# Moving the start addresses of SBUF tiles in a two-block transformer kernel: the small-column pool ahead of the split-weight pool, and filler tiles in three places

## The chip, the cores and the metric

The kernel runs on one core of a Trainium2 chip. The metric is the device time in microseconds (us) of one execution. Three executions of the kernel before gave 2179.43 us (median), from 2176.91 to 2179.5. The execution that was profiled took 2180.57 us, and its trace spans 2178.5 us of that.

## The reference

The input is 256 tokens of width 1024 in float32. Two layers and a further block follow each other:

```python
for layer in range(DEPTH):                 # DEPTH = 2
    mixer = hgrn_gmlp_mixer if layer % 2 == 0 else mla_moba_mixer
    x = x + mixer(x, *mixer_params[layer])
    x = x + peer_ffn(x, *ffn_params[layer])
...
def peer_ffn(x, norm_ffn, w_query, sub_keys, expert_down, expert_up):
    ...
        q = (xi @ w_query).reshape(B, PEER_CHUNK, PEER_HEADS, 2, PEER_HALF)
        s = jnp.einsum('bthpd,hpnd->bthpn', q, sub_keys)
        ...                                # two top-16, then the top 16 of the pairs
        u = jnp.take(expert_down, idx, axis=0)
        act = jax.nn.gelu(jnp.einsum('btd,bthkd->bthk', xi, u).astype(jnp.float32))
        v_sel = jnp.take(expert_up, idx, axis=0)
        return jnp.einsum('bthk,bthkd->btd', (g * act).astype(xi.dtype), v_sel)
```

Each peer layer has 16,384 experts. The second block (`second_block`) normalises, multiplies by a wide input matrix, does a pooled branch and a dilated attention, and multiplies by two projections and an output matrix.

## The kernel before

**Products in three parts.** Every large matrix product is done on fp32r operands split into a high and a low part: `hi = copy(x)` on ScalarE (L487) and `lo = x - hi` on VectorE or GpSimd (L488), in `split_weights`. A product then takes three matmuls (hi·hi, hi·lo, lo·hi, in `mm3`), so TensorE reads two SBUF operands for each: the stationary one, 128 columns (512 bytes of a partition), which a weight load brings in, and the moving one, 256 or 512 columns. All of them are issued from one line, L421.

**Peer layers.** The kernel doesn't gather experts. It takes all 128 blocks of 128 experts in turn. For each block `project` multiplies the block's down weights by the normalised tokens: 24 matmuls, named `ps<-xh,wh`, `ps<-xl,wh`, `ps<-xh,wl` in the trace, with the weights stationary and the tokens (`xh`, `xl`) moving, 256 columns. `expand` multiplies the gated activations by the block's up weights: 12 matmuls, `acc<-wh,W` and `acc<-wl,W`, with the activations `W` stationary and the weights moving, 512 columns. Per layer the stretches are: the query product (`acc<-xh,w`, `acc<-xl,w`) with the top-16 searches on VectorE and the first 40 projections between them; the gate matrices from one-hot products in fp16 (`acc<-oo,ah`) with 60 more projections; 124 expansions, into whose last part the other 28 projections are put one by one; and 4 expansions from tiles named `places`. The order within a stretch is written out by the program, partly by a count of costs (class `Balance`), and is fixed before the run.

**Mixers and second block.** Their products stream through the class `Stream`: a piece of 1024 weight columns is loaded into `wraw`, split, and used. In "T" jobs the weights are stationary and the tokens move (`acc<-xh,wh`); in "N" jobs the tokens are stationary and the weights move (`acc<-wh,xh`, 256 or 512 columns). The mixers put some split pieces in their own pool (`w`, names `wh` and `wl` as well) and some in the shared pool `ws`.

**Pools.** SBUF is given out in the order in which pools are opened. The outer order is constants (with `xh` and `xl`), `raw` (4 tiles of 4096 bytes), `ws` (5 pairs `wh`, `wl` of 4096 bytes each), `esm` (four tags of one or a few columns), and then what each stage opens. In a peer layer's front that is `small`, `wraw`, `tmp` and `w` (the split query weights); in the second block `first`, `wraw`, `small`, `mg` (two tiles), `act` and `wk`. A tile takes its bytes rounded up to 32.

Of the kernel before, what the change touches and what calls it, by code (L numbers as in the profile page):

```python
# [7 lines left out]
F32 = mybir.dt.float32  # L8
# [101 lines left out]
class Lin:  # L110
# [5 lines left out]
    def __init__(self, x, W, nk, cols, cn, kind, cb, late=0, k0=0, acc=None, start=True, stop=True,  # L116
                 need=None, mid=None, of=None, pieces=None):
        self.x, self.W, self.nk, self.cn, self.kind, self.cb, self.late = x, W, nk, cn, kind, cb, late
        self.mid, self.of = mid, of
        self.pieces = pieces or range({"T": cn // 128, "N": 2, "N2": 4}[kind])  # L120
        self.k0, self.acc, self.start, self.stop, self.need = k0, acc, start, stop, need
        self.cols = cols if isinstance(cols, tuple) else (cols, cn, 1, cn)
        self.w, self.keep = [], False
        if of:
            of.keep = True
# [240 lines left out]
class Net:  # L366
    def __init__(self, ctx, tc, A):
        self.tc, self.nc, self.A, self.ctx = tc, tc.nc, A, ctx
        nc = self.nc
        P = lambda name, **k: ctx.enter_context(tc.tile_pool(name=name, **k))  # L370
        self.cp = P("consts", bufs=1)
        self.raw = P("raw", bufs=4)
        self.dram = P("dram", bufs=1, space=DRAM)
        self.n = 0
        cp = self.cp
        self.ws = P("ws", bufs=WS)
        self.pa = P("pa", bufs=4, space=PSUM)
        self.pb = P("pb", bufs=4, space=PSUM)
        self.esm = P("esm", bufs=1)
        self.xn = [cp.tile([128, KB, S], F32R, name=n) for n in ("xh", "xl")]  # L380
        self.ident = cp.tile([128, 128], F32, name="ident")
        nc.scalar.dma_start(self.ident, A["c_ident"])
        self.vec = cp.tile([128, NVEC], F32, name="vec")
        self.entry = self.brow = None
# [701 lines left out]
    def peer(self, l, nxt, parity):  # L1086
# [8 lines left out]
        T = lambda pool, shape, dt, name, tag=None, **k: pool.tile(shape, dt, name=self.uid(name), tag=tag or name, **k)  # L1095
        with ExitStack() as outer:
# [49 lines left out]
            with ExitStack() as ctx:  # L1146
                P = lambda name, **k: ctx.enter_context(tc.tile_pool(name=self.uid(name), **k))
# [76 lines left out]
                def pair_top(tb):  # L1224
# [15 lines left out]
                        hs = range(h, h + 4)  # L1240
                        yield from best16([CV[:, j] for j in hs], [CI[:, j] for j in hs], [cand[:, j] for j in hs], 112)
                    gt = T(tmp, [128, 8, 16], F32, "gt")
                    gs = T(self.sm, [128, 8], F32, "gs")
                    nc.vector.tensor_tensor(gt, CV, CV[:, :, 0:1].to_broadcast([128, 8, 16]), op=OP.subtract)
                    nc.scalar.activation(gt, gt, AF.Exp)

# [47 lines left out]
                def front():  # L1294
# [51 lines left out]
                    for tb in range(2):  # L1346
                        yield from pair_top(tb)
# [23 lines left out]
            with ExitStack() as ctx:  # L1371
                P = lambda name, **k: ctx.enter_context(tc.tile_pool(name=self.uid(name), **k))
# [201 lines left out]
    def block2(self, out):  # L1574
# [5 lines left out]
                    pass  # L1580
        with ExitStack() as ctx:
            P = self.open(ctx)
            xp = P("mg", bufs=1)
            a = P("act", bufs=1)
            wk = P("wk", bufs=2)
            W = A["w_in_2"][0]
# [300 lines left out]
```

## Time and profile before

| | |
|---|---|
| median of three executions | 2179.43 us |
| the profiled execution | 2180.57 us |
| its span in the trace | 2178.5 us |
| TensorE busy | 2122.6 us, 97% |
| VectorE busy | 1568.8 us, 72% |
| ScalarE busy | 1125.7 us, 52% |
| GpSimd busy | 215.7 us, 10% |
| mean DMA rate | 175 GB/s |
| granted TensorE clock, mean | 0.994 |

Busy times are of the engine, and can hide spacing: matmuls are pipelined, and a matmul's own time in the trace is longer than the distance to the next one. So for TensorE the distance between the starts of two matmuls that follow each other says what one costs, and it is read from the view of instructions in order of time. "PEld" is the weight load, which overlaps the matmuls.

### The profile page before, as it was taken

The page shows a single profiled execution, that of the slowest core. Times are in us where ns is not written, and L with a number is a line of the kernel's source. Part 1 is how long each engine was busy: PE and PEld are TensorE (multiplying, and loading weights), DVE is VectorE, ACT ScalarE, POOL GpSimd, SP SyncE. Part 2 cuts the span into 40 slices and gives each one's busy share as a digit, 9 for nine tenths or more (in the row PEclk, how much of TensorE's full clock was granted, in tenths as well). Part 3 has the DMA queues.
Part 4 walks back from the last instruction along what each step waited for, and adds up shares of the span by engine and source line. Part 5 has one row for each costly group of instructions (what it writes and reads, how often), then busy time and mean ns, then how long its engine had stood idle before and what let it go on. Part 6 is the DMA issues. An engine that isn't in the chain of part 4 may idle for free.

```text
span 2178.5 us, 37618 instructions
## 1 busy us (share of the span) xinstructions
PE 2122.6 (97%) x14793; PEld 1932.1 (89%) x14793; DVE 1568.8 (72%) x2898; ACT 1125.7 (52%) x1944; POOL 215.7 (10%) x133
## 2 busy tenths in 40 slices
PE   7899999999999999998999999999999999999998
PEld 6879999999888888987799999998888889899998
DVE  7968978997555565668679789986666656644565
ACT  6245655554444444557455655555555555554443
POOL 2520110000000000013202200000000000122223
PEclk9999999999999999999999999999999999999999
DMA  7555454455666665744264545446666657475443
GB/s 233 185 185 184 145 194 146 156 159 161 188 189 190 188 195 192 260 129 148 87 233 135 195 149 162 155 155 188 189 187 190 194 193 261 148 218 153 136 146 115
DMA packets 165581, 382.19 MB, mean 175 GB/s; under 512 B 13137, under 2 KB 82444, under 8 KB 165148
## 3 DMA queue, kind: packets, MB, share of 16 engines
q1 hardware_dynamic: 160544, 364.95, 53.0%
q0 software_dynamic: 4672, 14.76, 1.9%
q8 instruction: 116, 1.90, 0.4%
q14 instruction: 61, 0.50, 0.1%
q10 hardware_dynamic: 188, 0.09, 0.0%
HBM read 376.56 MB, written 8.43 MB: 177 GB/s over the span
## 4 chain that ended last, share of the span: by engine, by line
PE 86%; DVE 9%; ACT 3%; issue 1%; DMA 0%; DVEq 0%; ACTq 0%
PE acc L421 53%; PE ps L421 29%; DVE wl L488 2%; ACT wh L487 1%; PE bsc L421 1%; PE bo L421 1%; DVE qL L678 1%; PE ps L200 1%; PE sc L421 0%; PE bpt L1747 0%; DVE eq L1278 0%; DVE s L1195 0%; DVE CI L1200 0%; DVE SC L658 0%; ACT scr L873 0%
## 5 line engine op out<-in xcount | busy, mean ns | idle before, releaser
L488 DVE TENSOR_TENSOR wl<-raw,wh 128x1024 fp32r<-128x1024 f32 x484 | 600.0, 1249 | 135.2 <-ACT wh L487 134.4
L421 PE MATMUL acc<-wh,W 128*128 128x512 f32 x1984 | 630.8, 395 | 0.0
L421 PE MATMUL ps<-xh,wh 128*128 128x256 f32 x2048 | 579.1, 283 | 0.0
L421 PE MATMUL ps<-xl,wh 128*128 128x256 f32 x2048 | 572.9, 280 | 0.0
L421 PE MATMUL ps<-xh,wl 128*128 128x256 f32 x2048 | 572.6, 280 | 0.0
L487 ACT ACTIVATE wh<-raw 128x1024 fp32r<-128x1024 f32 x504 | 526.9, 1054 | 74.2 <-PE ps L421 55.4
L421 PEld LDWEIGHTS acc<-wh,W 128*128 128x128 f32 x1984 | 373.4, 188 | 85.6 <-DVE W L1431 0.4
L421 PE MATMUL acc<-wl,W 128*128 128x512 f32 x992 | 391.5, 395 | 0.0
L421 PEld LDWEIGHTS ps<-xh,wh 128*128 128x128 f32 x2048 | 385.2, 188 | 2.4
L421 PEld LDWEIGHTS ps<-xl,wh 128*128 128x128 f32 x2048 | 385.1, 188 | 2.1
L421 PEld LDWEIGHTS ps<-xh,wl 128*128 128x128 f32 x2048 | 385.2, 188 | 0.0
L421 PEld LDWEIGHTS acc<-wl,W 128*128 128x128 f32 x992 | 186.7, 188 | 42.0 <-DVE wl L488 0.3
L1430 ACT ACTIVATE W<-ZB 128x256 fp32r<-128x256 f32 x168 | 91.4, 544 | 184.7 <-PE acc L421 161.0
L487 ACT ACTIVATE wh<-wraw 128x1024 fp32r<-128x1024 f32 (+1 forms) x140 | 144.4, 1043 | 46.5 <-PE acc L421 38.2
L1431 DVE TENSOR_TENSOR W<-ZB,W 128x256 fp32r<-128x256 f32 x168 | 89.8, 534 | 108.4 <-ACT W L1430 108.4
L488 DVE TENSOR_TENSOR wl<-wraw,wh 128x1024 fp32r<-128x1024 f32 (+2 forms) x104 | 132.8, 1284 | 45.9 <-ACT wh L487 45.7
L421 PE MATMUL acc<-xh,wh 128*128 128x256 f32 x480 | 136.2, 284 | 0.0
L421 PE MATMUL acc<-xh,wl 128*128 128x256 f32 x480 | 133.4, 278 | 0.0
L421 PE MATMUL acc<-xl,wh 128*128 128x256 f32 x480 | 133.3, 278 | 0.0
L181 POOL TENSOR_TENSOR ZB<-X,gain 128x512 f32<-128x512 f32 x4 | 5.2, 1293 | 1293.9 <-ACT ZB L179 1293.9
L1474 ACT ACTIVATE ZB<-acc 128x352 f32<-128x352 f32 (+30 forms) x128 | 47.7, 373 | 123.1 <-PE acc L421 119.3
L421 PE MATMUL acc<-wh,xh 128*128 128x256 f32 (+2 forms) x336 | 107.9, 321 | 0.9 <-ACT scr L873 0.9
(409 smaller groups left out, 3114.2 us busy)
## 6 DMA issues: line engine op xcount, KB each, us to landing
raw<-in_l_down_t_dram SPq DMA_DIRECT2D x256, 512.0 KB, 4.3
raw<-in_l_peer_expert_up_dram SPq DMA_DIRECT2D x248, 512.0 KB, 4.3
wraw<-in_l_w_in_dram SPq DMA_DIRECT2D x36, 512.0 KB, 5.1
wraw<-in_w_in_dram SPq DMA_DIRECT2D x36, 512.0 KB, 3.9
wraw<-in_l_peer_w_query_dram SPq DMA_DIRECT2D x32, 512.0 KB, 5.3
wraw<-in_w_in_dram SPq DMA_DIRECT2D x48, 256.0 KB, 3.3
wraw<-in_l_w_out_dram SPq DMA_DIRECT2D x16, 512.0 KB, 4.2
brow<-row POOLq DMA_DIRECT2D x1, 5120.0 KB, 33.6
```

Source lines behind the costliest of these rows:

```text
L181: nc.gpsimd.tensor_tensor(y, x, self.gB[:, ns], op=OP.mult)
L200: nc.tensor.transpose(q[:, k * 128:k * 128 + 128], self.work[tb][:, (k0 + k) * 128:(k0 + k) * 128 + 128], self.net.ident)
L421: self.nc.tensor.matmul(*a, **k)
L487: self.nc.scalar.activation(hi, r, AF.Copy)
L488: (eng or self.nc.vector).tensor_tensor(lo, r, hi.bitcast(F32), op=OP.subtract)
L678: nc.vector.tensor_tensor(qL, q, Wt, op=OP.mult)
L1430: nc.scalar.activation(h, act, AF.Copy)
L1431: nc.vector.tensor_tensor(l, act, h.bitcast(F32), op=OP.subtract)
L1474: nc.scalar.activation(ZB[:, f - E0:, t4], pv[:, f:], AF.Copy, scale=1.0 / GSC)
```

## The change

Nothing is added to or taken from the instructions, and on no engine does one stand in another place. What changes is where tiles lie in SBUF.

```diff
         cp = self.cp
+        self.esm = P("esm", bufs=1)
         self.ws = P("ws", bufs=WS)
         self.pa = P("pa", bufs=4, space=PSUM)
         self.pb = P("pb", bufs=4, space=PSUM)
-        self.esm = P("esm", bufs=1)
...
-                    gs = T(self.sm, [128, 8], F32, "gs")
+                    gs = T(self.sm, [128, 32], F32, "gs")[:, :8]
...
             P = self.open(ctx)
+            P("gap1", bufs=1).tile([128, 48], F32, name="gap1")
             xp = P("mg", bufs=1)
+            P("gap2", bufs=1).tile([128, 96], F32, name="gap2")
             a = P("act", bufs=1)
```

The pool `esm` takes 128 bytes of a partition, so `ws` starts 128 bytes later, and what is behind both stays. `gs` has four buffers in `small`, each now 128 bytes and not 32: what is opened behind `small` in a peer layer's front moves by 384 bytes. In the second block `mg` moves by 192 bytes, and `act` and `wk` by 576. The first bytes in the built programs, and what is left of them after division by 256 (the "offset" below):

| tiles | before | after | offset before | offset after |
|---|---|---|---|---|
| `xh`, `xl` | 16512, 24704 | same | 128 | 128 |
| `raw` (4) | 33600 and on | same | 64 | 64 |
| `ws`: `wh`, `wl` | 49984 and on | 50112 and on | 64 | 192 |
| `W` (activations) | 135104, 137152 | same | 192 | 192 |
| `places` | 91072 | same | 192 | 192 |
| mixers' pool `w` | 134080 and on | same | 192 | 192 |
| query weights `w` | 196672 and on | 197056 and on | 64 | 192 |
| `mgh`, `mgl` | 124480, 132672 | 124672, 132864 | 64 | 0 |
| `bh`, `bl`, `yh`, `yl` | 157248 and on | 157824 and on | 64 | 128 |

Every piece of these tiles that a matmul reads starts a multiple of 256 bytes behind the tile's start, so the offset is that of each operand.

## Rows read from the trace of the kernel before

**Rows 1.** The page: busy time of the engines, and the last chain's shares.

```profile
PE 2122.6 (97%) x14793; PEld 1932.1 (89%) x14793; DVE 1568.8 (72%) x2898; ACT 1125.7 (52%) x1944; POOL 215.7 (10%) x133
...
PE 86%; DVE 9%; ACT 3%; issue 1%; DMA 0%; DVEq 0%; ACTq 0%
```

**Rows 2.** Groups by shape on TensorE: count | busy us, mean ns | idle before.

```profile
L421 PE MATMUL acc<-wh,W 128*128 128x512 f32 x1984 | 630.8, 395 | 0.0
L421 PE MATMUL ps<-xh,wh 128*128 128x256 f32 x2048 | 579.1, 283 | 0.0
...
L421 PE MATMUL acc<-xh,wh 128*128 128x256 f32 x480 | 136.2, 284 | 0.0
...
L421 PE MATMUL acc<-wh,xh 128*128 128x256 f32 x256 | 74.9, 293 | 0.9 <-ACT scr L873 0.9
...
L421 PE MATMUL acc<-xh,w 128*128 128x256 f32 x384 | 71.1, 281 | 0.0
```

**Rows 3.** Stretches: length, busy PE, PEld, DVE, ACT, POOL (count), clock, DMA share, GB/s.

```profile
200.00:300.00 100.00, 94.11 (x789) 93.56 (x787) 95.48 (x337) 53.93 (x76) 19.27 (x7) 0.98 0.43 138
...
350.00:500.00 150.00, 150.00 (x1457) 149.00 (x1455) 139.00 (x233) 78.67 (x183) 0.00 (x0) 1.00 0.50 156
...
560.00:800.00 240.00, 240.00 (x1035) 194.58 (x1034) 142.20 (x173) 117.67 (x172) 0.00 (x0) 1.00 0.62 189
...
810.00:940.00 130.00, 130.00 (x836) 117.42 (x835) 79.32 (x98) 65.96 (x96) 0.00 (x0) 1.00 0.66 217
...
1940.00:2100.00 160.00, 159.34 (x1274) 147.84 (x1273) 85.44 (x142) 78.24 (x137) 36.78 (x20) 1.00 0.51 150
```

**Rows 4.** Waits of TensorE: total us, times, longest.

```profile
PE ps L1267 <- DVE gt L1264: 7.4, 4, 2.4
```

**Rows 5.** In order of time, TensorE: start us, own us; projections, 42 spacings apart.

```profile
401.00 0.28 PE L421 MATMUL ps<-xl,wh 128*128 128x256 f32 x1
...
405.95 0.28 PE L421 MATMUL ps<-xl,wh 128*128 128x256 f32 x1
```

**Rows 6.** The same view, first mixer, weights from pool `w`: 47 spacings apart.

```profile
29.36 0.28 PE L421 MATMUL acc<-xh,wh 128*128 128x256 f32 x1
...
34.69 0.28 PE L421 MATMUL acc<-xh,wl 128*128 128x256 f32 x1
```

**Rows 7.** Second mixer, N job; weights of `ws`, then from 991.25 of `w`: 6, 11 spacings.

```profile
990.57 0.28 PE L421 MATMUL acc<-wh,xh 128*128 128x256 f32 x1
...
991.25 0.28 PE L421 MATMUL acc<-wh,xh 128*128 128x256 f32 x1
...
992.55 0.28 PE L421 MATMUL acc<-wh,xl 128*128 128x256 f32 x1
```

**Rows 8.** Expansions, 66 spacings from the first row's start to the last's.

```profile
589.64 0.62 PE L421 MATMUL acc<-wh,W 128*128 128x512 f32 x2
...
604.97 0.40 PE L421 MATMUL acc<-wh,W 128*128 128x512 f32 x1
```

**Rows 9.** The last expansions of a layer, from `places`: start, length of all, count.

```profile
1883.94 9.70 PE L421 MATMUL acc<-places 128*128 128x512 f32 x42
```

**Rows 10.** Second block's end: projections (15 spacings), then a T job (47).

```profile
2137.10 0.28 PE L421 MATMUL acc<-bh,wh 128*128 128x256 f32 x1
...
2138.90 0.28 PE L421 MATMUL acc<-xh,wh 128*128 128x256 f32 x1
...
2144.44 0.28 PE L421 MATMUL acc<-xh,wl 128*128 128x256 f32 x1
```

**Rows 11.** Projections in the first layer's search stretch, 76 spacings.

```profile
290.01 0.28 PE L421 MATMUL ps<-xl,wh 128*128 128x256 f32 x1
...
298.63 0.28 PE L421 MATMUL ps<-xh,wl 128*128 128x256 f32 x1
```

**Rows 12.** Groups on VectorE: the split in `ws`, and in `places`.

```profile
L488 DVE TENSOR_TENSOR wl<-raw,wh 128x1024 fp32r<-128x1024 f32 x484 | 600.0, 1249 | 135.2 <-ACT wh L487 134.4 <-PE ps L421 0.3
...
L488 DVE TENSOR_TENSOR places<-ZB,places 128x1024 fp32r<-128x1024 f32 x8 | 9.8, 1219 | 0.0
```

## The prediction

> **What bounds the kernel now.** I read the page first: TensorE is busy for 97% of the span, and 86% of the chain that ended last runs on it [rows 1]. Then the view by stretches [rows 3]: in the gate stretch (350 to 500), the expansions (560 to 800), the alternating stretch (810 to 940) and the second block (1940 to 2100) TensorE is busy throughout or nearly, and VectorE is busy for 139.00 of 150, 142.20 of 240, 79.32 of 130 and 85.44 of 160 us. So there a cheaper matmul shortens the run. In the search stretch (200 to 300) it is otherwise: VectorE 95.48 of 100 us, TensorE 94.11, and TensorE waits for search results there, the gates `gt` for example [rows 4].
>
> The view that decides this case is TensorE's in order of time. No instruction changes place, so the change can act only through addresses, and addresses differ already within the kernel before. With "difference" I mean the stationary operand's offset less the moving one's, modulo 256 bytes. Matmuls of 256 columns at steady spacing, with offsets from the table of the change:
>
> - moving 128, stationary 64, difference 192: 4.95 us for 42 spacings, 117.9 ns [rows 5]
> - moving 128, stationary 192, difference 64: 5.33 us for 47, 113.4 ns [rows 6]
> - moving 64, stationary 64, difference 0: 1.80 us for 15, 120.0 ns; the T job right behind it (difference 192) takes 5.54 us for 47, 117.9 ns [rows 10]
> - in one unbroken chain, weights of `ws` (moving 64, stationary 128, difference 64) run at 0.68 us for 6, 113.3 ns, and the next unit, from pool `w` (moving 192, difference 192), at 1.30 us for 11, 118.2 ns [rows 7]
>
> With 512 columns: the expansions (moving 64, stationary 192, difference 128) take 15.33 us for 66, 232.3 ns [rows 8]; those from `places` (both 192, difference 0) take 9.70 us for 42, and less the last one's own 0.39 us (as long as the 395 ns of the others of this shape), 9.31/41 = 227.1 ns [rows 2, 9].
>
> So the spacing follows the difference, though not it alone: the same addresses that give 117.9 ns once ran for 76 spacings at 8.62/76 = 113.4 ns [rows 11]. A chain of matmuls falls into one step or the other when it starts and tends to keep it; the difference sets which step it mostly ends in.
>
> The other engines show nothing like this: VectorE's split takes a mean of 1249 ns in `ws` and 1219 ns in `places`, whose tiles lie at another offset [rows 12], 2% apart. I cost VectorE, ScalarE, GpSimd and the DMAs at nothing; they are covered by TensorE outside the search stretch in any case.
>
> **The change part by part.** It removes and adds no instruction and no wait. The counts are from rows 2 and the loops.
>
> 1. Expansions: `ws` goes to 192, the difference from 128 to 0, the pair of offsets that `places` has. Two of three read `wh`, so 1984 × 3/2 = 2976 matmuls [rows 2], each 232.3 − 227.1 = 5.2 ns cheaper: 15.5 us. VectorE's 142.20 of 240 us leave this room.
> 2. Projections: 3 × 2048 = 6144 [rows 2], from difference 192 to 64, the pair of rows 6: at most 117.9 − 113.4 = 4.5 ns each. Some already run fast [rows 11], and some chains will stay slow, so I take 3.5 ns in long chains. The gate stretches hold 2 × 60 × 24 = 2880: 10.1 us. VectorE limits this: 150 us there become 150 − 1080 × 0.0035 = 146.2 for TensorE (some 1080 of the 1457 matmuls are projections; the rest are fp16 and don't change), against 139.00 on VectorE [rows 3]; it fits with 5% left, and I keep 90%: 9.1 us. The alternating stretches hold 2 × 28 × 24 = 1344 in chains of 24, which start anew at each expansion: 1344 × 3.1 = 4.2 us. The search stretches hold 2 × 40 × 24 = 1920, and with the query products, which move in the same way (1.5 × 384 = 576) [rows 2], 2496 × 3.5 = 8.7 us. There VectorE sets the pace, so a faster TensorE mostly waits earlier for `gt`; I keep 40%: 3.5 us.
> 3. T jobs, nearly all in the second block: 3 × 480 less 144 that read pool `w` is 1296, from difference 192 to 64. Their bounds are 0 (they already run fast) and 1296 × 4.5 = 5.8 us; stretches of both kinds stand in the trace, so half: 2.9 us.
> 4. The second block's projections and output product: 2 × 192, from difference 0 to 64 (`bh`, `yh` moving at 128; `mg` stationary at 0 under `ws` at 192): 120.0 − 113.4 = 6.6 ns, 2.5 us. That is what the two fillers there are for.
> 5. Against it: N jobs on `ws` go from difference 64 to 192, as in rows 7. Of the 3 × 256 [rows 2] 408 read `ws`: at most 408 × 4.9 = 2.0 us dearer, and since some are slow now, I take 1.3 us. 240 of 512 or 448 columns make the same move; no row shows that. Their bound is the spread of rows 8 and 9, 5.2 ns either way, ±1.2 us; I take 0.
> 6. Mixers' output products that move `ws` weights past tokens at 192: about 138 × 5.2 = 0.7 us cheaper, as in 1. The fp32 transposes are too few to count (±0.3 us).
>
> The sum: 15.5 + 9.1 + 4.2 + 3.5 + 2.9 + 2.5 − 1.3 + 0.7 = 37.1 us. From the profiled 2180.57 us (span 2178.5 and 2.1 around it), which lies 1.1 us above the median of 2179.43, that gives 2143.5, and from the median 2142.3. I say 2142.
>
> **The rivals.**
>
> *Addresses make no difference; the spacings come from the kind of job.* For it: each class of offsets belongs to other operations, and rows 11 run fast without any change. Against it: in rows 7 one job, one shape and one chain change step with the buffer alone. It would give 2179. The Trainium skill has the rule behind this rival: SBUF — State Buffer, section "Who interferes with whom", gives TensorE two independent read ports, one for the moving operand and one for weight loads, and says "PE and ACT never wait on anyone". By that rule the sum is zero; rows 7 disagree with it by 4.9 ns a matmul.
>
> *Only part of it arrives.* Chains stay in the slow step (in chains of 24 and 48 that start anew after the fp16 products or an expansion), or VectorE takes over: at 139.00 of 150 us [rows 3] the rise of its share late in the gate stretch could meet TensorE's new pace. Then parts 2 and 3 give about 4 us together, and the others stay: 15.5 + 4 + 2.5 + 0.7 − 1.3 = 21.4, thus 2158.
>
> *All of it arrives.* Every chain of the gate and alternating stretches and of the T jobs ends in the fast step, (2880 + 1344 + 1296) × 4.5 = 24.8 us, and half of the search stretch's 2496 × 4.5 counts, 5.6 us, with parts 1, 4, 5, 6 as above: 15.5 + 24.8 + 5.6 + 2.5 − 1.3 + 0.7 = 47.8, thus 2132.
>
> *Slower.* Difference 0 is the worst one at 256 columns [rows 10]; `places` may be fast for how its chain is entered [rows 9], as rows 11 are. If an expansion paid at 512 columns what 256 columns pay twice, 2 × 120.0 = 240.0 ns, 2976 × 7.7 = 22.9 us would be added. With chains that keep their step (parts 2 and 3 at 0) only part 4 stands against it: 2179.4 + 22.9 − 2.5 = 2200. It decides once the expansions' spacing is over 232.3 + 2.5/2.976 = 233.1 ns and the projections don't move. Against it: the 42 of rows 9 hold 227.1 ns as a whole, first ones included, at both operands' new offsets.
>
> **How the numbers follow.** The forecast 0.71; part of it 0.14; all of it 0.05; no difference 0.06; slower 0.04. A measurement of this kernel can tell about 0.2%, 4.4 us, from no change. Faster by more than that is 0.90, within it 0.06, slower 0.04. The range from 2131 to 2157 takes in the forecast with its bounds (parts 2 and 3 between half and all), the case of all, and not quite that of part; outside lie the other cases and about 0.06 of the forecast's own, together close to 0.2. All cases but two are of one sign, so one range is enough.
>
> **What would show it.** In the profile after, expansions should stand 227 ns apart, and the 240 us from 560 hold about 1035 × 232.3/227.1 = 1059 matmuls; projections in the gate stretch 113 to 114 ns apart, with a few chains at 118; the second block's `acc<-wh,mgh` at 113 in place of 120; N jobs on `ws` at 118. The waits for `gt` and for search results should grow, since TensorE arrives earlier: that is where part 2 loses its 60%. VectorE's busy time should stay within 1%. I am wrong in part 1 if expansions stay over 230 ns; in part 2 if most long chains of projections stay at 118, or if TensorE waits for VectorE in the gate stretch; and wrong altogether if all spacings stay as they are.

## The result, and the profile after

The changed kernel takes 2153.68 us (median of four, 2152.74 to 2157.69) against 2179.47 for the kernel before (four, 2176.91 to 2179.76): the ratio is 0.9888, 95% interval 0.9871 to 0.9905, so 25.8 us faster. The forecast was 2142 with a range from 2131 to 2157: sign and range hold, 11.3 of the 37.1 us did not come.

The page of the changed kernel, busy times and the last chain's shares, and its groups by shape on TensorE and VectorE (count | busy us, mean ns | idle before), against [rows 1, 2, 12]:

```profile
PE 2104.1 (98%) x14793; PEld 1930.2 (90%) x14793; DVE 1565.5 (73%) x2898; ACT 1124.5 (52%) x1944; POOL 217.9 (10%) x133
...
PE 86%; DVE 10%; ACT 3%; issue 1%; DMA 0%; ACTq 0%; DVEq 0%
...
L488 DVE TENSOR_TENSOR wl<-raw,wh 128x1024 fp32r<-128x1024 f32 x484 | 598.6, 1246 | 137.4 <-ACT wh L487 136.3
L421 PE MATMUL acc<-wh,W 128*128 128x512 f32 x1984 | 619.5, 389 | 0.0
L421 PE MATMUL ps<-xh,wh 128*128 128x256 f32 x2048 | 582.1, 284 | 0.0
```

The work on every engine is the same, and TensorE is busy for 18.5 us less, the other engines for at most 3.3 us less: the larger of the expansions' two groups gives 11.3 of the 18.5, the projections' group shown here nothing. VectorE's split kept its time (1249 and 1246 ns).

Stretches of the changed kernel (columns as in [rows 3]):

```profile
560.00:780.00 220.00, 220.00 (x972) 182.24 (x971) 133.62 (x162) 110.57 (x162) 0.00 (x0) 1.00 0.64 194
350.00:500.00 150.00, 150.00 (x1459) 148.93 (x1458) 138.80 (x231) 78.25 (x183) 0.00 (x0) 1.00 0.51 158
```

The kernel before has 949 matmuls between 560 and 780 us:

```profile
560.00:780.00 220.00, 220.00 (x949) 178.36 (x948) 130.16 (x159) 108.10 (x158) 0.00 (x0) 1.00 0.62 188
```

972 in place of 949 is a step shorter by 2.4%, as from 232.6 to 227 ns. In the gate stretch 1459 stand where 1457 stood: next to nothing moved there. The instructions in order of time (start, own time) say the same. The changed kernel's expansions, 69 spacings:

```profile
589.03 0.62 PE L421 MATMUL acc<-wh,W 128*128 128x512 f32 x2
...
604.67 0.62 PE L421 MATMUL acc<-wh,W 128*128 128x512 f32 x2
```

15.64/69 = 226.7 ns, 232.3 in [rows 8]. A pair of projections in its gate stretch, from the fp16 products to the next ones:

```profile
403.26 1.09 PE L421 MATMUL acc<-oo,ah 128*128 128x128 f16 x16
404.16 0.36 PE L421 MATMUL ps<-xh,wh 128*128 128x256 f32 x1
404.36 0.28 PE L421 MATMUL ps<-xl,wh 128*128 128x256 f32 x1
...
409.77 0.28 PE L421 MATMUL ps<-xh,wl 128*128 128x256 f32 x1
409.90 1.09 PE L421 MATMUL acc<-oo,ah 128*128 128x128 f16 x16
```

From 404.36 to 409.77 are 46 spacings, 117.6 ns: the step of [rows 5], with the addresses of [rows 6], which ran at 113.4. And in the search stretch of the same trace, at the same addresses, two chains follow each other:

```profile
284.70 0.28 PE L421 MATMUL ps<-xh,wl 128*128 128x256 f32 x1
...
295.25 0.28 PE L421 MATMUL ps<-xh,wl 128*128 128x256 f32 x1
296.89 0.41 PE L1289 MATMUL ps<-ident,sel 128*128 128x128 f32 x2 [1.37 <-DVE sel L1283]
...
297.38 0.28 PE L421 MATMUL ps<-xh,wl 128*128 128x256 f32 x1
...
322.46 0.28 PE L421 MATMUL ps<-xh,wl 128*128 128x256 f32 x1
```

93 spacings in 10.55 us are 113.4 ns; then, after a pause and two transposes, 213 in 25.08 us are 117.7. So at difference 64 both steps exist, as they do at 192 [rows 5, 11].

Summed over every matmul of a kind, the time from its start to the next start went so (us, before to after; only spacings without a gap are compared in parts 5 and 6):

| part of the prediction | forecast | in the traces |
|---|---|---|
| 1 expansions | -15.5 | 692.5 to 675.2: -17.3 |
| 2 projections and query | -16.8 | 742.8 to 741.7 and 68.5 to 67.3: -2.3 |
| 3 T jobs | -2.9 | 172.2 to 171.3: -0.9 |
| 4 second block | -2.5 | 46.4 to 45.0: -1.4 |
| 5 N jobs | +1.3 | 768 x (116.6 - 116.1 ns) = +0.4; of 512 or 448 columns 213 x (224.0 - 227.0) = -0.6 |
| 6 mixers' output products | -0.7 | 160 x (228.3 - 231.7) = -0.5 |

Together -22.6, and the span went from 2178.5 to 2155.6, -22.9. The profiled execution is the longest of its four (2157.69), so the traces hold 22.9 of the median's 25.8 us. The gaps that parts 5 and 6 leave out moved single groups by up to 3.5 us, both ways, and all but cancel.

### The profile page after: what moved, and what is told of

The parts are those of the page before. It is cut to its first block, busy times and chain, and to the rows that moved or that the text cites. A ratio compares the mean times of both kernels' runs of the same rounds, so it can differ in the third digit from the quotient of the medians.

```text
span 2155.6 us, 37618 instructions
## 1 busy us (share of the span) xinstructions
PE 2104.1 (98%) x14793; PEld 1930.2 (90%) x14793; DVE 1565.5 (73%) x2898; ACT 1124.5 (52%) x1944; POOL 217.9 (10%) x133
## 4 chain that ended last, share of the span: by engine, by line
PE 86%; DVE 10%; ACT 3%; issue 1%; DMA 0%; ACTq 0%; DVEq 0%
PE acc L421 53%; PE ps L421 29%; DVE wl L488 3%; ACT wh L487 1%; PE bsc L421 1%; PE bo L421 1%; DVE qL L678 1%; PE ps L200 1%; PE sc L421 0%; DVE s L1195 0%; PE lev L421 0%; PE bpt L1749 0%; DVE CI L1200 0%; ACT scr L873 0%; ACT TF L1227 0%
## 5 line engine op out<-in xcount | busy, mean ns | idle before, releaser
L488 DVE TENSOR_TENSOR wl<-raw,wh 128x1024 fp32r<-128x1024 f32 x484 | 598.6, 1246 | 137.4 <-ACT wh L487 136.3
L421 PE MATMUL acc<-wh,W 128*128 128x512 f32 x1984 | 619.5, 389 | 0.0
L421 PEld LDWEIGHTS ps<-xl,wh 128*128 128x128 f32 x2048 | 390.5, 191 | 2.0
L421 PE MATMUL acc<-wl,W 128*128 128x512 f32 x992 | 386.0, 389 | 0.0
L488 POOL TENSOR_TENSOR wl<-wraw,wh 128x1024 fp32r<-128x1024 f32 (+1 forms) x36 | 87.0, 2418 | 222.8 <-ACT wh L487 215.5
```

Source lines behind the costliest of these rows:

```text
L421: self.nc.tensor.matmul(*a, **k)
L488: (eng or self.nc.vector).tensor_tensor(lo, r, hi.bitcast(F32), op=OP.subtract)
```

## The experiments

Theory A is the prediction's: the difference sets the spacing. Theory C: the difference sets which steps there are, and what TensorE does ahead of a chain sets which of them it takes. Rivals: addresses don't matter; the absolute place matters; the place in the program does. A "chain" is a run of projections with nothing else between; "slow" and "fast" are its steps of 117.7 and 113.4 ns. One trace of each kernel was kept, so whether a kernel takes the same steps in every execution no run shows.

**Which edit brings the gain.** `ws_only` has the pool's move alone:

```diff
+        self.esm = P("esm", bufs=1)
         self.ws = P("ws", bufs=WS)
...
-        self.esm = P("esm", bufs=1)
```

> The change with only the pool of short columns moved in front of the split weights; gs keeps its 8 columns and the second block has no fillers. Theory A (the spacing of 512-column matmuls follows the difference of the operands' start offsets, and the expansions go from 128 to 0): the 2976 expansions run at 227 ns again instead of 232.6, about -17 us, and the projections hardly move, so about -19 to -22 us of the change's -25.8: near 2158 us against 2179. Theory B (the fillers carry a good part of the gain): at most -15 us, above 2164. In both the projections stay near 117.5 ns.

Measured: 2154.85 us, ratio 0.9893 (0.9875 to 0.9910); expansions 226.8 ns, projections 116.8.

`rest_only` has the rest:

```diff
+                    gs = T(self.sm, [128, 32], F32, "gs")[:, :8]
...
+            P("gap1", bufs=1).tile([128, 48], F32, name="gap1")
+            P("gap2", bufs=1).tile([128, 96], F32, name="gap2")
```

> The change without the move of the pool: only gs padded and the two fillers in the second block. Theory A: the output projection of the second block (mgh, 192 matmuls) goes from 120 to 114 ns, 192 x 6 ns = -1.2 us, the query weights from 117.8 to 115.7, about -1.1 us, the expansions stay at 232.6: together -2 to -4 us, 2175 to 2178. Theory B (the fillers matter more): -8 us or more, below 2172.

Measured: 2175.45 us, ratio 0.9985 (0.9976 to 0.9995): 3.1 us. `mg` products 120.0 to 114.2 ns, query 115.3, expansions 232.7. The pool's move carries nearly all.

**The projections' difference alone.** Five kernels keep the changed one's split weights and all behind them in place and move `xh` and `xl`, by putting `vec` (192 bytes) or column tiles (32 bytes each) in front of them. The identity of the few transposes moves along, and `raw` by up to 128 bytes, which TensorE doesn't read; VectorE's split from it kept 1245 to 1250 ns in all five. `x128`:

```diff
+        self.vec = cp.tile([128, NVEC], F32, name="vec")
         self.xn = [cp.tile([128, KB, S], F32R, name=n) for n in ("xh", "xl")]
...
-        self.vec = cp.tile([128, NVEC], F32, name="vec")
```

> The changed kernel with the tile vec in front of xh and xl: these two move by 192 bytes and nothing else that TensorE reads does, so the difference of the projections (and of the other matmuls with xh, xl) goes from 64 to 128 and that of the expansions stays 0. Theory A (the step follows the difference alone): some one step for all 6144 projections, in which the chains behind the gate's fp16 matmuls and those elsewhere agree. Theory C (the difference says which steps there are, and what TensorE does ahead of a chain which of them it takes): again two kinds of chain, 113.4 and 117.8 ns, by what stands ahead of them, and the time within 3 us of 2154. If 128 were free of the slow step, 6144 x 4.2 ns less those already fast = about -23 us, 2131.

`x0` has this, and

```diff
+        self.esm = P("esm", bufs=1)
         self.cp = P("consts", bufs=1)
         self.raw = P("raw", bufs=4)
...
-        self.esm = P("esm", bufs=1)
         self.ws = P("ws", bufs=WS)
```

> As x128, with the pool of short columns also in front: xh and xl move by 320 bytes, the difference of the projections is 0, that of the expansions 0 as in the changed kernel. Theory A and C both: at difference 0 the 256-column matmuls had 120.0 ns in every chain of the second block's end, so 6144 x (120.0 - 117.4) = +16 us, and about +4 us from the other matmuls with xh, xl: about 2173. Rival (the addresses of 256-column matmuls don't count, the 120.0 came from elsewhere): 2154, with 117.5 in the projections.

`x32` puts only `ess` in front, `x96` `ess` and `vec`, `x224` `ess`, `ey` and `ea`:

```diff
+        self.esa = P("esa", bufs=1)
         self.cp = P("consts", bufs=1)
...
-        self.ss = net.esm.tile([128, 2, 2], F32, name=net.uid("ess"), tag="ess")
+        self.ss = net.esa.tile([128, 2, 2], F32, name=net.uid("ess"), tag="ess")
```

> As x96, with one column tile alone in front of xh and xl, difference 32. Theory C: a mean of its own between 113.4 and 120 ns, 2129 to 2179. Rival D (rounded to 64): as 0 or as 64, 120 or 117.5 ns, 2179 or 2154.

> The changed kernel with vec and one column tile (ess) in front of xh and xl, which move by 224 bytes: difference 96 in the projections and the other matmuls with xh, xl, 0 in the expansions as before. At 0 the runs showed one step of 120, at 64 two (113.4 and 117.7), at 128 steps around 119. Theory C (the difference says which steps there are): again mostly one pattern of steps of its own, mean between 113.4 and 120; at 113.4 throughout, the time would be 2154 - 6144 x 4.0 ns = 2129, at 120 2179. Rival D (only multiples of 64 bytes count, offsets are rounded): 96 reads as 64 or as 128, means 117.5 or 119.1, 2154 or 2173.

> As x96, with three column tiles in front of xh and xl, difference 224. Theory C: a mean of its own between 113.4 and 120 ns, 2129 to 2179. Rival D (rounded to 64): as 192 or as 0, 117.6 or 120 ns, 2154 to 2179.

Measured, with the changed kernel and the kernel before beside them (mean of the projections' spacings under 160 ns):

| kernel | difference | time, us | spacing, ns | chains |
|---|---|---|---|---|
| `x0` | 0 | 2178.97 | 119.9 | all alike, 120 |
| `x32` | 32 | 2169.11 | 118.3 | alike, mixed steps of 115 to 123 |
| after | 64 | 2153.68 | 117.4 | 113.4 or 117.7 |
| `x96` | 96 | 2166.59 | 118.6 | mixed steps of 115 to 122, means of 118.6 and 118.7 behind expansions and fp16 |
| `x128` | 128 | 2172.67 | 119.1 | means of 119.8 behind expansions, 118.6 behind fp16 |
| before | 192 | 2179.47 | 117.6 | 113.4 or 117.7 |
| `x224` | 224 | 2158.02 | 116.9 | 116 or 117 behind expansions and fp16, mixed in the search |

A pair in the gate stretch of `x0`, to be compared with that of the changed kernel above:

```profile
403.83 1.09 PE L421 MATMUL acc<-oo,ah 128*128 128x128 f16 x16
...
404.93 0.28 PE L421 MATMUL ps<-xl,wh 128*128 128x256 f32 x1
...
410.44 0.28 PE L421 MATMUL ps<-xh,wl 128*128 128x256 f32 x1
410.56 0.23 PE L421 MATMUL acc<-oo,ah 128*128 128x128 f16 x1
```

46 spacings in 5.51 us, 119.8 ns. Moving the two tiles of tokens cost 25.3 us, without an instruction changed. That addresses don't matter falls, and so does rounding to 64 bytes (32 and 96 are each unlike their neighbours). Theory A falls in its strong form: at 64, and at 192, two steps live side by side, and at 128 the mean goes with what stands ahead. Theory C's forecast for `x128`, the two steps of 64 again and a time within 3 us of 2154, missed too: each difference has steps of its own.

**Difference or place.** `w192` starts the split weights 64 bytes lower than the changed kernel does:

```diff
         self.ws = P("ws", bufs=WS)
+        self.esm2 = P("esm2", bufs=1)
...
-        y, a = (self.esm.tile([128, 1], F32, name=self.uid(t), tag=t) for t in ("ey", "ea"))
+        y, a = (self.esm2.tile([128, 1], F32, name=self.uid(t), tag=t) for t in ("ey", "ea"))
```

> The changed kernel with only two of the four column tiles in front of the split weights, which so lie 64 bytes lower than in the changed kernel: difference 64 in the expansions and 0 in the projections, with wh and xh both at 128 mod 256 (x0 had both at 192). Theory A for the expansions (the step follows the difference): 2976 expansions at about the 233 ns of the few 512-column matmuls at difference 64, so +18 us, and the projections at 120.0 as in x0, +16 us: about 2190. Rival (the absolute place counts, not the difference): projections not at 120.0, or expansions at 227.

Measured: 2193.37 us, ratio 1.0066 (1.0043 to 1.0089). Its expansions, 60 spacings in 14.00 us, 233.3 ns:

```profile
589.72 0.39 PE L422 MATMUL acc<-wh,W 128*128 128x512 f32 x1
...
603.72 0.39 PE L422 MATMUL acc<-wh,W 128*128 128x512 f32 x1
```

Its projections, both operands at 128, stand 119.7 ns apart, 119.9 in `x0` with both at 192. The expansions alone could still follow the place of `ws`, for their `W` never moved. The N jobs of 512 columns settle it: their spacings have a median of 227 ns in `w192` (both operands at 128) and in `x0` (both at 192), of 233 before (difference 64) and 229 after (192). The difference counts, not the place. Its period is 256 bytes as far as seen: `wh` starts 33,280 bytes behind `xh` in `x0` and 33,536 in `w192`, 130 and 131 times 256, and the projections run alike.

**What sets a chain's step.** `split_first`, at the changed kernel's addresses, writes each projection's first matmul as two:

```diff
+                self.mm(pP[:, :128], dh[:, 0], xh[:, 0, :128], start=True, stop=False)
+                self.mm(pP[:, 128:], dh[:, 0], xh[:, 0, 128:], start=False, stop=False)
```

> The changed kernel, addresses as there, with the first matmul of each of the 256 projections of the gate and expansion stretches written as two of 128 columns. Theory C (the chain's entry decides which of the two steps at difference 64 it takes): part of the 64 chains behind the gate's fp16 products, all of which ran at 117.7 ns, now run at 113.4; if all do, 2688 x 4.2 ns = -11 us less the second start of each projection, 256 x some 60 ns = 15 us at most, so 2140 to 2165, and the spacing in 400 to 500 us tells. Theory E (the step is set by the place in the program, such as what DVE and ACT do at the time, not by the entry): 117.7 everywhere in the gate stretch still, and only the 256 extra starts, 2154 to 2170.

Measured: 2167.61 us, ratio 0.9949 (0.9926 to 0.9972). One gate pair of it, first the projection behind the fp16 products, then the second one:

```profile
406.87 0.42 PE L421 MATMUL ps<-xh,wh 128*128 128x128 f32 x2
...
407.30 0.28 PE L421 MATMUL ps<-xh,wl 128*128 128x256 f32 x1
...
409.77 0.28 PE L421 MATMUL ps<-xh,wl 128*128 128x256 f32 x1
409.89 0.34 PE L421 MATMUL ps<-xh,wh 128*128 128x128 f32 x2
...
410.70 0.28 PE L421 MATMUL ps<-xh,wh 128*128 128x256 f32 x1
...
412.63 0.28 PE L421 MATMUL ps<-xh,wl 128*128 128x256 f32 x1
```

2.47/21 = 117.6 ns ahead of the second split and 1.93/17 = 113.5 behind it, in one chain. All 64 projections right behind fp16 products stayed slow; all 124 split within a chain, and 49 of 50 behind expansions, where 49 of 50 are slow in the changed kernel, ran fast. So it is the entry, not the place in the program. The time alone would not have told: it lies in theory E's range, since a split was taken at some 60 ns and cost 118 to 188 ns behind expansions and in the gate (means by place).

"Entry" is more than which instructions stand ahead, though. `ws_only` has the changed kernel's instructions and addresses for every projection, and its chain behind the same wait and the same two transposes as in the search stretch above, where the changed kernel took 117.7 ns, is fast:

```profile
296.57 0.41 PE L1289 MATMUL ps<-ident,sel 128*128 128x128 f32 x2 [1.37 <-DVE sel L1283]
...
297.06 0.28 PE L421 MATMUL ps<-xh,wl 128*128 128x256 f32 x1
...
321.20 0.28 PE L421 MATMUL ps<-xh,wl 128*128 128x256 f32 x1
```

213 spacings in 24.14 us are 113.3 ns. Of the 18 chains in the search stretches 16 are fast in `ws_only`, 5 in the changed kernel, 2 in `rest_only` and 2 before. What decides there stays open.

`kick_sizes` asks whether a cheaper split exists (`kick` and `at` differ from place to place):

```diff
+                    if kick and k == at:
+                        for c, d in ((0, kick), (kick, S)):
+                            self.mm(pP[:, c:d], dh[:, k], xh[:, k, c:d], start=k == 0 and c == 0, stop=False)
```

> The changed kernel with one matmul split in two in 32 of the gate's 64 pairs or more (the second weight tile of the first projection behind the fp16 products) and in five of six of the expansions' projections (their first matmul), the first piece 128, 192, 224, 240, 64 or 32 columns wide in turn. Theory C (an irregular entry sets the step for the whole chain behind it): the gate's chains turn from 117.7 to 113.4 ns behind the split, with a cost of about 0.10 us a split at 128 columns as in split_first, and perhaps less at another width: 64 chains x (46 x 4.2 ns - 105 ns) = -5.6 us, the expansions' chains about even, so 2146 to 2156. Theory F (only a split at 128 columns does it): the other widths leave 117.7 and the time is 2153 to 2165.

Measured: 2156.04 us, ratio 0.9893 (0.9865 to 0.9922). Fast chains behind the split, by the first piece's width: in the gate, where the split matmul is the chain's fourth, 32: 10 of 10, 64: 10 of 10, 128: 12 of 12, 192: 0 of 12, 224: 10 of 10, 240: 10 of 10; behind expansions, where it is the first, 32: 8 of 8, 64: 1 of 10, 192: 8 of 8, 224 and 240: 0 of 16. Two neighbours between expansions, 192 and then 224 columns:

```profile
807.04 0.30 PE L421 MATMUL ps<-xh,wh 128*128 128x192 f32 x2
...
807.84 0.28 PE L421 MATMUL ps<-xh,wh 128*128 128x256 f32 x1
...
809.77 0.28 PE L421 MATMUL ps<-xh,wl 128*128 128x256 f32 x1
809.88 0.39 PE L421 MATMUL acc<-wh,W 128*128 128x512 f32 x1
...
812.61 0.29 PE L421 MATMUL ps<-xh,wh 128*128 128x224 f32 x2
...
813.42 0.28 PE L421 MATMUL ps<-xh,wh 128*128 128x256 f32 x1
...
815.43 0.28 PE L421 MATMUL ps<-xh,wl 128*128 128x256 f32 x1
815.54 0.40 PE L421 MATMUL acc<-wh,W 128*128 128x512 f32 x1
```

From the eighth start to the last, 17 spacings take 1.93 us and 2.01 us, 113.5 and 118.2 ns: the same work at the same addresses, and only the entry differs. Theory F falls. The whole chain takes 2.84 and 2.93 us, so a fast chain of 24 just pays for its split (2.83 us for a slow one in the changed kernel); by width, a split cost 0.10 to 0.14 us, once 0.20.

`turned` adds no instruction and lets one matmul of a chain take its columns in another order:

```diff
+                        turn = lambda t: t.rearrange("p (a b c) -> p b a c", b=step, c=2)
+                        self.mm(turn(pP), dh[:, k], turn(xh[:, k]), start=k == 0, stop=False)
```

> The changed kernel with no instruction added: at the same places as in kick_sizes one matmul of the chain reads its 256 moving columns, and writes its outputs, in another order (pairs of columns taken 2, 4, 8, 16, 32 or 64 pairs apart, in turn), all else as in the changed kernel. If such a matmul is irregular enough to move a chain from 117.7 to 113.4 ns and costs less than the 0.11 us of a split, 64 x 46 x 4.2 ns = 12 us and 48 x 23 x 4.2 ns = 5 us are to be had: down to 2139 if all turn at no cost. If the order of the columns leaves the reads' timing as it is, nothing turns: 2154. If reading pairs apart is slow itself (twice the time of a matmul, 112 x 0.11 us), up to 2166 without any turn.

Measured: 2156.64 us, ratio 0.9898 (0.9856 to 0.9941). In the gate 53 of 54 chains turned fast for steps of 2 to 32 pairs and 0 of 10 for 64, but where a chain turned, such a matmul and its successors cost 0.12 to 0.19 us more, as much as a split; the projections' sum stayed at 741.6 us.

`kick_best` splits only where a long chain follows:

```diff
+                    if kick and k == 1:
+                        self.mm(pP[:, :224], dh[:, k], xh[:, k, :224], start=False, stop=False)
+                        self.mm(pP[:, 224:], dh[:, k], xh[:, k, 224:], start=False, stop=False)
```

> The changed kernel with one matmul split into 224 and 32 columns, in 62 places: the second weight tile of the first of two projections behind the gate's fp16 products (54) and of the first of a run of projections in the search (8). In kick_sizes such a split cost 0.113 us over a fast chain and turned 10 chains of 10. Theory C: 54 x (46 x 4.3 ns - 113 ns) = -4.6 us and in the search 8 x -113 ns + 960 x 4.3 ns = -3.2 us, together -7.8 us against the changed kernel: 2146, ratio to the kernel before 0.985. If the time on TensorE is given back by what feeds it (DVE was 73% busy): 2150 to 2154.

Measured: 2151.91 us, ratio 0.9871 (0.9855 to 0.9888), and 0.9888 (0.9871 to 0.9905) for the changed kernel: the two can't be told apart by time. A gate pair of it:

```profile
404.24 0.29 PE L421 MATMUL ps<-xh,wh 128*128 128x224 f32 x2
...
405.05 0.28 PE L421 MATMUL ps<-xh,wh 128*128 128x256 f32 x1
...
409.36 0.28 PE L421 MATMUL ps<-xh,wl 128*128 128x256 f32 x1
409.47 0.23 PE L421 MATMUL acc<-oo,ah 128*128 128x128 f16 x1
```

38 spacings in 4.31 us, 113.4 ns; behind the split 59 of 62 chains are fast, all 56 in the gate (the expectation counted 54) and 3 of 6 in the search. From one group of fp16 products to the next are 6.57 us and not 6.64: 54 x 0.07 = 3.8 us, nearly all of the 4.2 by which the projections' sum fell (741.7 to 737.5). The 3.2 us expected in the search did not come, and that sum can fall as far without a split: it is 737.5 in `ws_only`, too, by its search chains. Whether the 4.2 us reach the median stays open: it fell by 1.8, less than the intervals.

## Why the prediction was partly right

**Part 1 was right.** The expansions went to 226.8 ns, forecast 227.1, and gave 17.3 us for 15.5; they had been at 232.6 on average, a little over [rows 8]. The rival "slower", that difference 0 might cost 512 columns what it costs 256, fell.

**Part 2 is the step that failed:** 2.3 us for 16.8. Its own sign of being wrong came: most long chains stayed at 118 ns. The prediction said that the difference sets which step a chain "mostly ends in", and took 3.5 of 4.5 ns. It had compared chains that were entered in different ways: [rows 5] stand behind fp16 products, [rows 6] in a mixer's stream. At 64 and at 192 the same two steps exist; behind the gate's fp16 products 63 of 64 chains are slow before and 64 of 64 after, behind expansions 49 of 50 after. [Rows 11], where the old addresses ran fast, had shown this. The working noted it and still gave the rival "part of it", which named these very chains and priced them at 21.4 us, a chance of 0.14. That rival is what happened: -22.9 in the traces, with parts 2 and 3 at 3.2 us for its 4. The prediction's range left this rival out, at 2158; that 2153.68 lies in the range is in part luck.

**Part 3** gave 0.9 us for 2.9, for the same reason: 192 and 64 are alike, and half of these chains were fast already.

**Part 4** gave 1.4 for 2.5. At difference 0 every chain is near 120 ns however it is entered, so leaving it gains, but in full only where the chain then enters fast: `mg` products went from 120.0 to 114.2 ns, the two projections only to 117.8, and to 113.4 to 114.0 at the same addresses in `split_first` and the kernels that move `xh`, except `x32`.

**Parts 5 and 6** were within 1 us. In [rows 7] a chain left the fast step when it changed from one pool to the other; on the whole the N jobs lost 0.4 us, not 1.3.

**The waits for `gt` did not grow**, 6.7 us in the changed kernel against 7.4 [rows 4]. They are 6.7 in `ws_only` as well, where most search chains were fast, so that waits take back the gain of faster chains there, for which part 2 left out 60%, is not shown:

```profile
PE ps L1267 <- DVE gt L1264: 6.7, 4, 3.2
```

**The rival "addresses make no difference"** is refuted: 25.3 us lie between the changed kernel and `x0`, which differ only in where tiles begin. The Trainium skill, SBUF — State Buffer, section "Who interferes with whom", gives TensorE two independent read ports and says "PE and ACT never wait on anyone". With two independent reads the distance between the operands' starts should not matter; the traces disagree, with 119.9 ns at difference 0 and 117.4 at 64 for the same projections. Whether the two reads meet, and where, was not tried.

## What to carry to other kernels

Where TensorE sets the time, read the distances between matmul starts, not the busy times, and look at the two operands' start addresses modulo 256 before touching the schedule: one pool of 128 bytes moved 1% of this kernel. Compare only chains that are entered in the same way, and more than one of them; the same addresses can hold two steps, and an expected gain holds only for the step that the chain's entry leads to. Choose offsets for each shape apart: of the differences tried here, 0 was the best for 512 moving columns and the worst for 256.

## What the runs showed of the hardware

- With 512 columns the spacing is 226.8 ns at difference 0 (changed kernel), 233.5 at 64 (`w192`) and 232.6 at 128 (before), in the N jobs about 229 at 192 (changed kernel). With 256 columns it is 119.9 at 0 and, at 64 and 192, 113.4 or 117.7; no difference that was tried gave 113.4 throughout. Steps follow differences of 32 bytes, too.
- A chain keeps its step over hundreds of matmuls (213 spacings at 117.7 ns), and one irregular matmul inside it can move it from the slow step to the fast one: a piece of 192 columns does so behind an expansion (8 of 8) where one of 224 doesn't (0 of 8), and in the gate stretch, where it stands three matmuls further in, it is the other way round (0 of 12, 10 of 10).
- Splitting a matmul of 256 columns into 32 and 224 costs as much as into halves, some 0.13 us (`kick_sizes`): about a whole matmul more.
